# One decoder layer on one core: attention scores made for four heads at a time, value products in turns over two banks, the last result in two halves

## The chip, the cores and the metric

The kernel runs on one of the eight cores of a Trainium2 chip. The metric is the device time of one execution in microseconds (us). TensorE (PE) multiplies matrices, VectorE (DVE) and ScalarE (ACT) do elementwise work, GpSimd (POOL) does small arithmetic and issues the accumulating loads, SyncE (SP) issues the other loads and the stores. Each engine takes its instructions in the order in which they were written.

## What is computed

One layer on 256 tokens of width 1024, all in float32 (cut to what matters):

```
h = rms_norm(x, norm1_g); proj = h @ w_in
q, k, v, u = split(proj, [512, 1024, 1536])            # 8 heads of 64
q, k = rope(rms_norm(q, q_norm_g)), rope(rms_norm(k, k_norm_g))
p = softmax(where(key <= query, q @ k.T / 8, -inf))    # one block of 256 keys: causal attention
attn = p @ v
conv = silu(layer_norm(causal_depthwise_conv(glu(u + glu_b), dw_w) + dw_b))
x = x + concat(attn, conv) @ w_out
h = rms_norm(x, norm2_g)
y = x + (silu(h @ w_gate) * (h @ w_up)) @ w_down       # width 2816
```

## The kernel before

**Products and weights.** Each float32 product is made of three: both factors are split into a high part (`h`, rounded to 12 bits of mantissa) and a rest (`l`), and hi*hi, hi*lo and lo*hi are added in one PSUM bank. Weights come from memory as blocks `raw` (SP's queue); ACT writes `wh` (line 270), DVE writes `wl` (line 275), as pieces of 1024 columns, seven of which may be alive.

**Order.** Nothing is reordered by a scheduler: the program is recorded in the order in which Python writes it. The loop over the input projection has five chunks of 512 columns (k, q, gate, conv input, v), each with eight steps of six products (line 686, two banks `p`). At each step `step()` runs the side tasks that have become due, and `yield n` puts a task off by n steps; so what a task issues stands on every engine between the products of two steps.

**Attention.** `q_task` ends by spawning four `pair_task`s, three steps apart. A pair makes the scores `S` of two heads (line 525): for each head a 128x128 and a 128x256 product with 64 rows, the two heads in different halves of the rows of the array (64 rows x 128 columns) and in two banks (tag `s`, two buffers). One step later `head_task` masks (line 534, a custom DVE instruction that adds the mask, and reads out the row maximum `mx`), makes the bias `bi` (line 538, with `scq`, made by POOL), waits, lets ACT take exponentials `p` (line 543), DVE normalizes (`rec` line 549, `p` line 551), PE transposes (`pT`, line 555), ACT copies to `pTs` (line 557). The transposed `p` of all heads meet the values `vs` (lines 693 and 694, ACT) in `O` (line 706): 16 products of 64 columns each, the two heads of a pair in two halves of the columns of the array, pair after pair, token half after token half. `O` has a bank for four heads; `split` (lines 251 and 252) turns each bank into `mixh` and `mixl`.

**Behind it.** Convolution in a transformed domain (`hf`, `cv`), its normalization (`ln_task`, transposes `cT`), the output projection (`po`, line 724), second normalization with transposes `x2T`, the feed-forward part (`fg`, `U`, `V`, `W`, transposes `aT`), the down projection `pd`. The last four rows of `pd` are finished one output tile at a time; DVE adds the residual (`o`, line 953) and SP's queue stores it (line 954), four times 128x512.

**Banks.** PSUM has eight: tag `mm` four (`p`, `O`, `po`, `fg`, `pd`), `s` two (`S`, `hf`, `cv`, `U`, `V`), `t` two (transposes and others). A tile takes the buffer of its tag that was used longest ago, and its first writer waits until that one's last reader is done.

Of the kernel before, what the change touches and what calls it, by code (L numbers as in the profile page):

```python
# [8 lines left out]
F32 = mybir.dt.float32  # L9
# [4 lines left out]
ALU = mybir.AluOpType  # L14
AX = mybir.AxisListType

P = 128
D = 1024
T = 256
NT = T // P  # L20
KT = D // P
W = 512
H = 8
HD = 64
# [25 lines left out]
KT_WAIT = 3  # L50
S_WAIT = 4
LATE = (1, 5)
GLU0_WAIT = 3
L1 = 8
L2 = 28
# [135 lines left out]
def _build(nc, tc, t, ctx):  # L191
# [6 lines left out]
    early_ctx = ExitStack()  # L198
    early = early_ctx.enter_context(tc.tile_pool(name="early", bufs=1))

    def mm_bank(name, cols=512):
        return psum.tile([P, cols], F32, name=name, tag="mm", bufs=4)

    def t_bank(name, tag="t"):
        return psum.tile([P, 512], F32, name=name, tag=tag, bufs=2)

    def work(name, tag, bufs, shape=(P, W), dt=F32):
        return early.tile(list(shape), dt, name=name, tag=tag, bufs=bufs)
# [12 lines left out]
    def spawn(gen, wait=0):  # L221
        tasks.append([now[0] + wait, gen])
# [263 lines left out]
    def q_task(banks):  # L486
        kqT = keep.tile([P, 2, 4, T], F32, name="kqT", tag="x2T")
        G["kT"], G["qT"] = kqT[:, 0], kqT[:, 1]
        qr, totals = [], []
        for i in range(NT):  # L490
            t1, total = rope_half(banks[i], 0, i, "q")
            totals.append(total)
            qr.append(t1)
            if i == 0:
                yield Q_GAP
        spawn(transposed(qr, G["qT"], "q"), QT_WAIT)
        yield 1
        for i in range(NT):
            r3 = heads3(G["kr"][i])
            nc.vector.tensor_tensor(r3, r3, cqk[1][:, i, :, None].to_broadcast([P, H, HD]), op=ALU.mult)  # L500
        spawn(transposed(G["kr"], G["kT"], "k"), KT_WAIT)
        yield 1
        for total in totals:
            total()
        mean_square(0)
        root(late_part)
        G["scq"] = early.tile([P, NT, H], F32, name="scq")
        nc.gpsimd.tensor_scalar(G["scq"], cqk[0], HD ** -0.5, None, op0=ALU.mult)
        for name, shape in (("fwd", [P, 2, NT, T]), ("ends", [96, R3 - 1]), ("inv", [P, 2, 3, T])):
            tl = early.tile(shape, F32R, name=name)  # L510
            nc.gpsimd.dma_start(tl, t[name])
            G[name] = tl if name == "ends" else (tl[:, 0], tl[:, 1])
        yield S_WAIT
        G["sums"] = early.tile([P, NT, H], F32, name="sums")
        G["pT"] = [None] * H
        for j in range(H // 2):
            spawn(pair_task(j), 3 * j)

    def pair_task(j):

        banks = [t_bank(f"S{2 * j + a}", "s") for a in range(2)]
        for out, q, k in ((slice(0, P), slice(0, P), slice(0, P)), (slice(P, 3 * P), slice(P, T), slice(0, T))):
            for a in range(2):
                rows = slice(a * HD, (a + 1) * HD)
                nc.tensor.matmul(banks[a][:, out], G["qT"][rows, j, q], G["kT"][rows, j, k], start=True, stop=True)  # L525
        for a in range(2):
            spawn(head_task(2 * j + a, banks[a], a), 1)
        yield 0

    def head_task(h, S, odd):  # L530
        sm = work(f"sm{h}", "sm", 3, shape=(P, 3 * P))
        mx = work(f"mx{h}", "mx", 4, shape=(P, NT))
        for i in range(NT):
            nc.vector.tensor_tensor_reduce(out=sm[:, spl[i]], in0=S[:, spl[i]], in1=mask[:, spl[i]], op0=ALU.add,  # L534
                                           op1=ALU.max, scale=1.0, scalar=-3e38, accum_out=mx[:, i:i + 1])
        bi = work(f"bi{h}", "bi", 4, shape=(P, NT))
        scq = G["scq"]
        nc.vector.scalar_tensor_tensor(bi, mx, -1.0, scq[:, :, h], op0=ALU.mult, op1=ALU.mult)
        yield HEAD_EXP + odd
        p = work(f"p{h}", "p", 3, shape=(P, 3 * P))  # L540
        s = G["sums"][:, :, h]
        for i in range(NT):
            nc.scalar.activation(p[:, spl[i]], sm[:, spl[i]], AF.Exp, bias=bi[:, i:i + 1], scale=scq[:, i, h:h + 1],
                                 accum_out=s[:, i:i + 1])
        if h == H - 1:
            nc.scalar.activation(table, one, AF.Silu)
        yield 1
        rec = work(f"rec{h}", "rec", 2, shape=(P, NT))
        nc.vector.reciprocal(rec, s)
        for i in range(NT):  # L550
            nc.vector.tensor_scalar(p[:, spl[i]], p[:, spl[i]], rec[:, i:i + 1], 1.0, op0=ALU.mult, op1=ALU.mult)  # L551
        yield 3 if h in LATE else 2
        b = t_bank(f"pT{h}")
        for a in range(3):
            nc.tensor.transpose(b[:, a * P:(a + 1) * P], p[:, a * P:(a + 1) * P], ident)  # L555
        G["pT"][h] = work(f"pTs{h}", f"pTs{h}", 1, shape=(P, 3 * P))
        nc.scalar.activation(G["pT"][h], b[:, 0:3 * P], AF.Copy)
# [114 lines left out]
    after = (k_task, q_task, gate_task, conv_task, None)  # L672
    unit = 0
    for chunk in range(5):
        banks = [mm_bank(f"p{chunk}{i}") for i in range(NT)]
        for kt in range(KT):
            step()
            feed(unit // 2 + 1 if unit < L1 else (unit + 3) // 2 if unit < L2 else min(unit // 2 + 3, BEHIND))
            w = wtile(unit * W, W)
            unit += 1  # L680
            sls = [slice(i * P, (i + 1) * P) for i in range(NT)]
            order = [(i, a) for i in range(NT) for a in range(3)]
            if W_FIRST < unit <= SWAP:
                order = [(0, 0), (0, 2), (1, 0), (1, 2), (0, 1), (1, 1)]
            for i, a in order:
                nc.tensor.matmul(banks[i], (xh, xh, xl)[a][:, kt, sls[i]], w[a % 2], start=kt == 0 and a == 0,  # L686
                                 stop=kt == KT - 1 and a == 2 - (order[-1][1] == 1))
        if after[chunk]:
            spawn(after[chunk](banks))
# [4 lines left out]
    nc.scalar.activation(vs[:, 1, :], banks[1], AF.Copy, scale=rstd1[:, 1:2])  # L694
    G["third"]()
    mix = G["mix"] = [keep.tile([P, KT, T], F32R, name="mix" + s, tag="big_" + s) for s in "hl"]
    O = [None, None]
    for pair in range(H // 2):
        step()
        if pair % 2 == 0:  # L700
            O[pair // 2] = mm_bank(f"O{pair // 2}").rearrange("p (a q) -> p a q", a=2)
        for i in range(NT):
            for odd in range(2):
                h = 2 * pair + odd
                o = O[pair // 2][odd * HD:(odd + 1) * HD, pair % 2, i * P:]
                nc.tensor.matmul(o, vs[:, i, h * HD:(h + 1) * HD], G["pT"][h][:, i * T:i * T + T - i * P],  # L706
                                 start=i == 0, stop=i == 1)
        if pair % 2:
            sl = slice(pair - 1, pair + 1)
            split([m[:, sl, :] for m in mix], O[pair // 2], nc.vector)  # L710
    spawn(ln_task())


# [46 lines left out]
    for k in range(4):  # L760
        feed(at + LEAD)
        for i in range(NT):
            for n in range(2):
                if k == 0:
                    po[i, n] = mm_bank(f"po{i}{n}")
                product(po[i, n], [m[:, k, tok(i)] for m in mix], wpart(at, n), k == 0, False)
        at += 1
    early_ctx.close()
# [123 lines left out]

    def plain_unit(c, z, kh, half):
        if kh == half == 0:
            banks[z] = [mm_bank(f"fg{c}{z}{i}") for i in range(NT)]
        for k in (2 * half, 2 * half + 1):
            for i in range(NT):
                product(banks[z][i], [a[:, 4 * kh + k, tok(i)] for a in g], wpart(at, k % 2),
                        kh == k == 0, kh == 1 and k == 3)
        if kh == half == 1:  # L900
            if WIDTHS[c] == W:
                spawn((gate2_task, up2_task)[z](c, banks[z], W), EVICT)
            else:
                spawn(gate2_task(c, banks[0], T), EVICT)
                spawn(up2_task(c, banks[0], T), EVICT + 1)
# [19 lines left out]

    def row(f, i, n, w):
        if f == 0:
            pd[i, n] = mm_bank(f"pd{i}{n}")
        product(pd[i, n], [acts[:, z, f, tok(i)] for z in range(2)], w, f == 0, f == NF - 1)

    spawn(norm2_task(), SS_WAIT)
# [16 lines left out]
    for i in range(NT):  # L948
        for n in range(2):
            for f in range(NF - LAST, NF):  # L950
                row(f, i, n, wpart(last[f], n))
            o = late.tile([P, W], F32, name=f"o{i}{n}", tag="sum", bufs=4)
            nc.vector.tensor_tensor(o, pd[i, n], x2[:, i, n * W:n * W + W], op=ALU.add)
            nc.sync.dma_start(t["out"][i][:, n * W:n * W + W], o)


def _layout(a):
# [56 lines left out]
```

## Time and profile before

| what | us |
|---|---|
| time, median of 3 runs (lowest, highest) | 285.69 (285.67, 286.34) |
| time of the profiled execution | 285.98 |
| its span in the trace | 284.2 |
| PE busy | 278.0 |
| DVE busy | 238.6 |
| ACT busy | 189.0 |
| POOL busy | 30.5 |

The span runs from the program's first instruction to its last. The 1.78 us by which the profiled execution is longer than its span lie outside the program's instructions and are taken as fixed. A timeline row has: start, time from the first start to the last end, engine, line, operation, output<-inputs, shapes, how many instructions are merged in it, and in brackets the idle time of the engine before it with what ended it. A product's end is modelled and lies after the start of the next one, so distances on PE are counted from start to start. A float32 product (`S`, `O`) makes two records.

### The profile page before, as it was taken

The numbers are of one execution on the slowest core, as the hardware profiler recorded it, in microseconds if no ns is written. First come the engines' busy times: TensorE is split into PE (matmuls) and PEld (weight loads), VectorE is DVE, ScalarE is ACT, GpSimd is POOL, SyncE is SP. The second block draws the span as 40 slices with busy tenths as digits, with TensorE's granted clock in tenths as the row PEclk, the third lists the DMA queues.
The fourth block names the chain that finished last, engine by engine and source line by source line (L and its number), as shares of the span: only waits on it lengthen the run. The fifth ranks groups of instructions, "written<-read, shape, count | busy, mean of one in ns | idle before, by whom it ended". The sixth has DMA issues, their size and how long they took to land.

```text
span 284.2 us, 3708 instructions
## 1 busy us (share of the span) xinstructions
PE 278.0 (98%) x1302; PEld 226.2 (80%) x1302; DVE 238.6 (84%) x352; ACT 189.0 (67%) x280; POOL 30.5 (11%) x54
## 2 busy tenths in 40 slices
PE   8999999999999999999999999999999999999993
PEld 6878877778788888888888888888888888888882
DVE  3889994999994957999998999899997999977421
ACT  5868568978747778664887559765687459864300
POOL 0004565002000000001200112002110022000000
PEclk9999999999999999999999999999999999999999
DMA  7999957834643589247999699996599985900011
GB/s 250 412 414 335 406 187 257 283 138 128 279 149 148 187 302 399 107 191 204 255 254 367 253 211 192 357 423 206 93 212 423 383 158 95 344 12 2 0 74 75
DMA packets 12885, 65.12 MB, mean 229 GB/s; under 512 B 1825, under 2 KB 2433, under 8 KB 7106
## 3 DMA queue, kind: packets, MB, share of 16 engines
q1 hardware_dynamic: 9874, 54.93, 50.9%
q0 software_dynamic: 2848, 9.94, 18.6%
q8 instruction: 10, 0.16, 0.2%
q14 instruction: 9, 0.07, 0.1%
q10 hardware_dynamic: 144, 0.00, 0.0%
HBM read 63.63 MB, written 1.05 MB: 228 GB/s over the span
## 4 chain that ended last, share of the span: by engine, by line
PE 93%; DVE 3%; ACT 1%; issue 0%; DVEq 0%
PE pd L724 21%; PE p L686 16%; PE U L724 15%; PE fg L724 12%; PE po L724 8%; PE V L724 8%; PE W L724 4%; PE aT L805 2%; PE warm L339 1%; DVE wl L275 1%; PE O L706 1%; DVE p L551 1%; DVE sm L534 1%; PE pT L555 1%; PE S L525 1%; PE x2T L747 1%
## 5 line engine op out<-in xcount | busy, mean ns | idle before, releaser
L270 ACT ACTIVATE wh<-raw 128x1024 fp32r<-128x1024 f32 x114 | 117.7, 1057 | 35.8 <-DVE raw L269 20.1
L275 DVE TENSOR_TENSOR wl<-raw,wh 128x1024 fp32r<-128x1024 f32 x114 | 135.9, 1220 | 4.8 <-ACT wh L270 3.8
L724 PE MATMUL pd<-wh,act 128*128 128x512 f32 x176 | 58.0, 394 | 0.0
L724 PEld LDWEIGHTS pd<-wh,act 128*128 128x128 f32 x176 | 33.0, 188 | 6.8
L724 PE MATMUL pd<-wl,act 128*128 128x512 f32 x88 | 34.3, 389 | 0.0
L686 PE MATMUL p<-wh,xh 128*128 128x512 f32 x80 | 32.8, 410 | 0.0
L686 PE MATMUL p<-wh,xl 128*128 128x512 f32 x80 | 31.5, 393 | 0.0
L283 POOL DMA_DIRECT2D raw<-w x16 | 14.1, 880 | 158.4 <-PE fg L724 61.4
L724 PE MATMUL fg<-wh,g 128*128 128x512 f32 x96 | 30.4, 391 | 0.0
L686 PE MATMUL p<-wl,xh 128*128 128x512 f32 x80 | 26.7, 395 | 0.0
L724 PE MATMUL U<-wh,g 128*128 128x512 f32 x64 | 21.5, 393 | 0.0
L724 PEld LDWEIGHTS fg<-wh,g 128*128 128x128 f32 x96 | 18.0, 188 | 3.7
L269 DVE TENSOR_TENSOR raw<-raw,raw 128x1024 f32<-128x1024 f32 x16 | 19.5, 1219 | 0.1
L724 PEld LDWEIGHTS pd<-wl,act 128*128 128x128 f32 x88 | 16.6, 188 | 3.3
L724 PE MATMUL fg<-wl,g 128*128 128x512 f32 x48 | 18.7, 390 | 0.0
L686 PEld LDWEIGHTS p<-wh,xh 128*128 128x128 f32 x80 | 15.3, 191 | 3.7 <-issue 0.7
L686 PEld LDWEIGHTS p<-wl,xh 128*128 128x128 f32 x80 | 15.1, 189 | 3.4 <-DVE wl L275 0.4
L686 PEld LDWEIGHTS p<-wh,xl 128*128 128x128 f32 x80 | 15.1, 189 | 3.1
L808 ACT ACTIVATE act<-aT 128x512 fp32r<-128x512 f32 (+1 forms) x12 | 6.7, 560 | 12.8 <-PE aT L805 12.8
L724 PEld LDWEIGHTS U<-wh,g 128*128 128x128 f32 x64 | 12.0, 188 | 2.4
L724 PE MATMUL po<-wh,mixh 128*128 128x512 f32 x32 | 12.6, 395 | 0.0
L724 PE MATMUL po<-wh,mixl 128*128 128x512 f32 x32 | 12.5, 390 | 0.0
(184 smaller groups left out, 445.9 us busy)
## 6 DMA issues: line engine op xcount, KB each, us to landing
raw<-w SPq DMA_DIRECT2D x45, 1024.0 KB, 7.0
raw<-w POOLq DMA_DIRECT2D x16, 512.0 KB, 7.0
first<-first SPq DMA_DIRECT2D x8, 384.0 KB, 6.0
xtok<-xtok SPq DMA_DIRECT2D x2, 512.0 KB, 9.1
x<-xtok SPq DMA_DIRECT2D x2, 512.0 KB, 6.5
out<-o SPq DMA_DIRECT2D x4, 256.0 KB, 2.0
inv<-inv POOLq DMA_DIRECT2D x1, 768.0 KB, 9.5
c_glub<-glub SPq DMA_DIRECT2D x1, 512.0 KB, 10.1
```

The lines of the kernel that those rows point to most:

```text
L269: nc.vector.tensor_tensor(src, src, blocks[add][:, cut(a)], op=ALU.add)
L270: nc.scalar.activation(dst[0], src, AF.Copy)
L275: nc.vector.tensor_tensor(dst[1], src, dst[0].bitcast(F32), op=ALU.subtract)
L283: nc.gpsimd.dma_start(blocks[to][:, cut(a)], t["w"][more - 2][:, cut(a)], accum_op=ALU.add)
L339: nc.tensor.matmul(warm[:, 0:T], zeros[:, 0:P], zeros, start=True, stop=True)
L525: nc.tensor.matmul(banks[a][:, out], G["qT"][rows, j, q], G["kT"][rows, j, k], start=True, stop=True)
L534: nc.vector.tensor_tensor_reduce(out=sm[:, spl[i]], in0=S[:, spl[i]], in1=mask[:, spl[i]], op0=ALU.add, op1=ALU.max, scale=1.0, scalar=-3e ...
L551: nc.vector.tensor_scalar(p[:, spl[i]], p[:, spl[i]], rec[:, i:i + 1], 1.0, op0=ALU.mult, op1=ALU.mult)
L686: nc.tensor.matmul(banks[i], (xh, xh, xl)[a][:, kt, sls[i]], w[a % 2], start=kt == 0 and a == 0, stop=kt == KT - 1 and a == 2 - (order[-1] ...
L724: nc.tensor.matmul(bank, l, r, start=start and a == 0, stop=stop and a == 2, skip_group_check=on)
L805: nc.tensor.transpose(b[:, a, :], u[:, a * P:(a + 1) * P], ident)
L808: nc.scalar.activation(hi, b[:, 0:nf, :], AF.Copy)
```

## The change

- The four `pair_task`s become two `pairs_task`s, of four heads each, three steps apart. The second pair of heads in each takes its two banks from the tag `mm0`. The masks of four heads stand together, then their four biases. There are eight buffers each of `sm`, `mx` and `bi` (before 3, 4 and 4). `head_task` begins with the exponentials, and is put off so that ACT issues them at the same places as before.
- The tag `mm` with four buffers becomes `mm0` and `mm1` with two each. Chunks of the projection take them by turns, both `O` banks are of `mm1`, `po` of token half 0 of `mm0` and so on.
- `O`: both banks from the start, and of each turn first the four products of token half 0 (both banks), then those of half 1; both banks are split at the end.
- The last of the four output tiles is added and stored in two halves of 256 columns, the second half by ACT's queue.
- The buffer for descriptors of POOL's loads is set to 8192.

```diff
+SECOND = 3
+SCORES = 8
+SCRATCH = 8192
-    def mm_bank(name, cols=512):
-        return psum.tile([P, cols], F32, name=name, tag="mm", bufs=4)
+    def mm_bank(name, two):
+        return psum.tile([P, 512], F32, name=name, tag=f"mm{two}", bufs=2)
...
-        for j in range(H // 2):
-            spawn(pair_task(j), 3 * j)
+        spawn(pairs_task(0))
+        spawn(pairs_task(2), SECOND)
+        for h in range(H):
+            spawn(head_task(h), 3 * (h // 2) + h % 2 + HEAD_EXP + 1 + (h < 2))
+
+    def pairs_task(first):
+        banks = {}
+        for j in (first, first + 1):
             for a in range(2):
+                banks[2 * j + a] = t_bank(f"S{2 * j + a}", "s") if j == first else mm_bank(f"S{2 * j + a}", 0)
+            for out, q, k in ((slice(0, P), slice(0, P), slice(0, P)), (slice(P, 3 * P), slice(P, T), slice(0, T))):
+                for a in range(2):
+                    rows = slice(a * HD, (a + 1) * HD)
+                    nc.tensor.matmul(banks[2 * j + a][:, out], G["qT"][rows, j, q], G["kT"][rows, j, k],
+                                     start=True, stop=True)
+        yield 1
+        mx = {}
+        for h, S in banks.items():
+            sm = masked[h] = work(f"sm{h}", "sm", SCORES, shape=(P, 3 * P))
+            mx[h] = work(f"mx{h}", "mx", SCORES, shape=(P, NT))
+            for i in range(NT):
+                nc.vector.tensor_tensor_reduce(out=sm[:, spl[i]], in0=S[:, spl[i]], in1=mask[:, spl[i]], op0=ALU.add,
+                                               op1=ALU.max, scale=1.0, scalar=-3e38, accum_out=mx[h][:, i:i + 1])
+        for h in banks:
+            bias[h] = work(f"bi{h}", "bi", SCORES, shape=(P, NT))
+            nc.vector.scalar_tensor_tensor(bias[h], mx[h], -1.0, G["scq"][:, :, h], op0=ALU.mult, op1=ALU.mult)
         yield 0
...
-    for pair in range(H // 2):
+    O = [mm_bank(f"O{n}", 1).rearrange("p (a q) -> p a q", a=2) for n in range(2)]
+    for second in range(2):
         step()
...
+        for i in range(NT):
+            for n in range(2):
+                for odd in range(2):
+                    h = 4 * n + 2 * second + odd
...
+        step()
+    for n in range(2):
+        split([m[:, 2 * n:2 * n + 2, :] for m in mix], O[n], nc.vector)
...
-            nc.vector.tensor_tensor(o, pd[i, n], x2[:, i, n * W:n * W + W], op=ALU.add)
-            nc.sync.dma_start(t["out"][i][:, n * W:n * W + W], o)
+            parts = 2 if i and n else 1
+            for a in range(parts):
+                one = slice(a * W // parts, (a + 1) * W // parts)
+                all_ = slice(n * W + one.start, n * W + one.stop)
+                nc.vector.tensor_tensor(o[:, one], pd[i, n][:, one], x2[:, i, all_], op=ALU.add)
+                (nc.scalar if a else nc.sync).dma_start(t["out"][i][:, all_], o[:, one])
```

On PE, in chunk 3, before (`S_530` and `S_531` are heads 0 and 1, `S_570` and `S_571` heads 2 and 3; `pw` is a product of the convolution's taps):

```order
L433 MATMUL pw_527<-dws,tapr 128x512
L525 MATMUL S_530<-kqT 128x128
L525 MATMUL S_531<-kqT 128x128
L525 MATMUL S_530<-kqT 128x256
L525 MATMUL S_531<-kqT 128x256
L686 MATMUL p_509<-wh_409,xh 128x512
```

and now, with heads 2 and 3 as `S_536` and `S_537`:

```order
L436 MATMUL pw_527<-dws,tapr 128x512
L533 MATMUL S_530<-kqT 128x128
L533 MATMUL S_531<-kqT 128x128
L533 MATMUL S_530<-kqT 128x256
L533 MATMUL S_531<-kqT 128x256
L533 MATMUL S_536<-kqT 128x128
L533 MATMUL S_537<-kqT 128x128
L533 MATMUL S_536<-kqT 128x256
L533 MATMUL S_537<-kqT 128x256
L698 MATMUL p_509<-wh_409,xh 128x512
```

Heads 2 and 3 have moved up behind heads 0 and 1; in the same way heads 4 to 7 now stand where heads 2 and 3 stood, and nothing is left at the two later places.

On DVE, behind the masks of heads 0 and 1, before:

```order
L538 SCALAR_TENSOR_TENSOR bi_562<-mx_559,scq 128x2
L275 TENSOR_TENSOR wl_537<-raw_303,wh_536 128x1024
L549 RECIPROCAL rec_591<-sums 128x2
L551 TENSOR_SCALAR p_576<-p_576,rec_591 128x128
L551 TENSOR_SCALAR p_576<-p_576,rec_591 128x256
L534 ISA sm_598,mx_599<-S_570,c_mask 128x128
```

and now, behind the masks of heads 0 to 3 (`S_588` is head 4, `S_595` head 7, `rec_639` head 0):

```order
L541 ISA mx_571 128x1
L545 SCALAR_TENSOR_TENSOR bi_574<-mx_559,scq 128x2
L545 SCALAR_TENSOR_TENSOR bi_576<-mx_563,scq 128x2
L545 SCALAR_TENSOR_TENSOR bi_578<-mx_567,scq 128x2
L545 SCALAR_TENSOR_TENSOR bi_580<-mx_571,scq 128x2
L278 TENSOR_TENSOR wl_543<-raw_303,wh_542 128x1024
L541 ISA sm_615,mx_616<-S_588,c_mask 128x128
```

and, at the end of the masks of heads 4 to 7 that follow there,

```order
L541 ISA sm_627,mx_628<-S_595,c_mask 128x256
L541 ISA mx_628 128x1
L545 SCALAR_TENSOR_TENSOR bi_631<-mx_616,scq 128x2
L545 SCALAR_TENSOR_TENSOR bi_633<-mx_620,scq 128x2
L545 SCALAR_TENSOR_TENSOR bi_635<-mx_624,scq 128x2
L545 SCALAR_TENSOR_TENSOR bi_637<-mx_628,scq 128x2
L561 RECIPROCAL rec_639<-sums 128x2
```

All eight masks now stand ahead of the first normalization; in the rest of DVE's order nothing but masks and biases has gone.

On PE, the first value products, before (`pTs_649` and `pTs_696` are heads 0 and 1, `pTs_702` and `pTs_735` heads 2 and 3; 64x256 is token half 0, 64x128 half 1):

```order
L706 MATMUL O_905<-pTs_649,vs 64x256
L706 MATMUL O_905<-pTs_696,vs 64x256
L706 MATMUL O_905<-pTs_649,vs 64x128
L706 MATMUL O_905<-pTs_696,vs 64x128
L706 MATMUL O_905<-pTs_702,vs 64x256
```

and now (`pTs_790` and `pTs_825` are heads 4 and 5, in the other bank):

```order
L717 MATMUL O_897<-pTs_679,vs 64x256
L717 MATMUL O_897<-pTs_714,vs 64x256
L717 MATMUL O_898<-pTs_790,vs 64x256
L717 MATMUL O_898<-pTs_825,vs 64x256
L717 MATMUL O_897<-pTs_679,vs 64x128
```

The first product that reads the second half of `vs` has moved from the third to the fifth place.

More of the change, by code (lines that the diff above doesn't have):

```diff
@@ L515, in q_task @@
         G["pT"] = [None] * H
-        for j in range(H // 2):
-            spawn(pair_task(j), 3 * j)
-    def pair_task(j):
-        banks = [t_bank(f"S{2 * j + a}", "s") for a in range(2)]
-        for out, q, k in ((slice(0, P), slice(0, P), slice(0, P)), (slice(P, 3 * P), slice(P, T), slice(0, T))):
-            for a in range(2):
[L524 to L527, printed above, removed]
-        yield 0
@@ L530, in head_task @@
[L530 to L539, printed above, removed]
+        spawn(pairs_task(0))
@@ L540, in head_task @@
+    masked, bias = {}, {}
+    def head_task(h):
+        sm, bi, scq = masked[h], bias[h], G["scq"]
         p = work(f"p{h}", "p", 3, shape=(P, 3 * P))
@@ L674, in _build @@
     for chunk in range(5):
-        banks = [mm_bank(f"p{chunk}{i}") for i in range(NT)]
+        banks = [mm_bank(f"p{chunk}{i}", chunk % 2) for i in range(NT)]
         for kt in range(KT):
@@ L696, in _build @@
     mix = G["mix"] = [keep.tile([P, KT, T], F32R, name="mix" + s, tag="big_" + s) for s in "hl"]
-    O = [None, None]
-    for pair in range(H // 2):
+    O = [mm_bank(f"O{n}", 1).rearrange("p (a q) -> p a q", a=2) for n in range(2)]
+    for second in range(2):
         step()
-        if pair % 2 == 0:
-            O[pair // 2] = mm_bank(f"O{pair // 2}").rearrange("p (a q) -> p a q", a=2)
         for i in range(NT):
[L703 to L710, printed above, removed]
+            for n in range(2):
+                for odd in range(2):
+                    h = 4 * n + 2 * second + odd
+                    o = O[n][odd * HD:(odd + 1) * HD, second, i * P:]
+                    nc.tensor.matmul(o, vs[:, i, h * HD:(h + 1) * HD], G["pT"][h][:, i * T:i * T + T - i * P],
+                                     start=i == 0, stop=i == 1)
+        step()
+    for n in range(2):
+        split([m[:, 2 * n:2 * n + 2, :] for m in mix], O[n], nc.vector)
     spawn(ln_task())
@@ L764, in _build @@
                 if k == 0:
-                    po[i, n] = mm_bank(f"po{i}{n}")
+                    po[i, n] = mm_bank(f"po{i}{n}", i)
                 product(po[i, n], [m[:, k, tok(i)] for m in mix], wpart(at, n), k == 0, False)
@@ L894, in plain_unit @@
         if kh == half == 0:
-            banks[z] = [mm_bank(f"fg{c}{z}{i}") for i in range(NT)]
+            banks[z] = [mm_bank(f"fg{c}{z}{i}", z) for i in range(NT)]
         for k in (2 * half, 2 * half + 1):
@@ L927, in row @@
         if f == 0:
-            pd[i, n] = mm_bank(f"pd{i}{n}")
+            pd[i, n] = mm_bank(f"pd{i}{n}", 1 - i)
         product(pd[i, n], [acts[:, z, f, tok(i)] for z in range(2)], w, f == 0, f == NF - 1)
@@ L1004 @@
     arrays = {**_layout(inputs), **_constants()}
-    nc = _bacc.Bacc("TRN2", target_bir_lowering=False, num_devices=1)
+    nc = _bacc.Bacc("TRN2", target_bir_lowering=False, num_devices=1,
+                     dynamic_dma_scratch_size=SCRATCH)
     arrays = {k: np.ascontiguousarray(v) for k, v in arrays.items()}
```

## The prediction

> **What bounds the kernel now.** I read the page first, then PE's waits, then PE's timeline at the places that the change touches, then DVE and ACT there, and the end.
>
> ```profile
> PE 278.0 (98%) x1302; PEld 226.2 (80%) x1302; DVE 238.6 (84%) x352; ACT 189.0 (67%) x280; POOL 30.5 (11%) x54
> ...
> PE 93%; DVE 3%; ACT 1%; issue 0%; DVEq 0%
> ```
>
> ```profile
> PE S L525 <- DVE mx L534: 0.3, 1, 0.3
> ```
>
> ```profile
> 80.00:280.00 200.00, 199.28 (x912) 164.72 (x910) 170.28 (x201) 127.70 (x165) 14.08 (x16) 1.00 0.68 214
> ```
>
> PE is the bound from the first product to the last, at a granted clock of 1.00. Its waits for others sum to 0.3 us beside 1.0 us of start. So time is gained only by what PE does not have to do, and by the end behind its last product. DVE (170.28 of 200 us) and ACT (127.70) have spare time in the long second part, so a lead that PE wins early should last. The 98%, though, hide distances between products that are longer than a stream needs: those are what this change can remove.
>
> **Scores: what a pair costs.** PE's timeline around the four pairs and, last, around a transpose without scores. A plain 512-column product starts 0.23 after the one before (57.20 and 57.43 below); one behind a change of shape is late.
>
> ```profile
> 42.08 0.39 PE L433 MATMUL pw<-dws,tapr 96*128 96x512 f32 x1
> 42.40 0.93 PE L525 MATMUL S<-kqT 64*128 64x128 f32 x8
> 43.26 0.50 PE L686 MATMUL p<-wh,xh 128*128 128x512 f32 x1
> 43.59 0.40 PE L686 MATMUL p<-wh,xl 128*128 128x512 f32 x1
> ```
>
> ```profile
> 42.73 0.60 PE L525 MATMUL S<-kqT 64*128 64x256 f32 x4
> ...
> 42.94 0.38 PE L525 MATMUL S<-kqT 64*128 64x256 f32 x2
> ```
>
> ```profile
> 46.45 0.93 PE L525 MATMUL S<-kqT 64*128 64x128 f32 x8
> ...
> 51.07 0.61 PE L686 MATMUL p<-wl,xh 128*128 128x512 f32 x2
> 51.62 0.93 PE L525 MATMUL S<-kqT 64*128 64x128 f32 x8
> 52.47 0.55 PE L555 MATMUL pT<-c_ident,p 128*128 128x128 f32 x3
> ...
> 53.09 0.39 PE L686 MATMUL p<-wh,xl 128*128 128x512 f32 x1
> ...
> 57.20 0.39 PE L686 MATMUL p<-wl,xh 128*128 128x512 f32 x1
> 57.43 0.39 PE L686 MATMUL p<-wh,xl 128*128 128x512 f32 x1
> 57.75 0.48 PE L525 MATMUL S<-kqT 64*128 64x128 f32 x2
> 58.50 0.92 PE L525 MATMUL S<-kqT 64*128 64x128 f32 x6 [0.26 <-DVE mx L534]
> 59.35 0.55 PE L555 MATMUL pT<-c_ident,p 128*128 128x128 f32 x3
> ...
> 59.96 0.39 PE L686 MATMUL p<-wl,xh 128*128 128x512 f32 x1
> ...
> 62.27 0.39 PE L686 MATMUL p<-wh,xl 128*128 128x512 f32 x1
> 62.50 0.49 PE L555 MATMUL pT<-c_ident,p 128*128 128x128 f32 x3
> ...
> 63.06 0.39 PE L686 MATMUL p<-wl,xh 128*128 128x512 f32 x1
> ```
>
> First pair: from `pw` (42.08) to the second `p` behind the scores (43.59) are 1.51; without scores it would be two plain distances, 0.46. The pair costs 1.05. Of this, streaming is 0.63: the two passes over 256 columns start 0.21 apart (42.73, 42.94), so those over 128 columns need half, and each pass serves both heads at once, 2x0.21 + 2x0.105. The other 0.42 is the price of going into this shape of the array and out again: 0.09 ahead of the first score, 0.11 for its first weights, 0.11 behind the last, 0.11 at the first `p`. The second pair has the same row (0.93) and is taken as equal, 1.05. The third: 51.07 begins two products, so the stream without it goes on at 51.53; to 53.09 are 1.56, less the 0.56 that a transpose and a product take without scores (62.50 to 63.06): 1.00. The fourth: 57.66 to 59.96 are 2.30, less 0.56: 1.74. It stops in its middle, since head 7's bank is free only when DVE has masked head 5, and the two heads then no longer run side by side. Together 4.84.
>
> Now there are two groups of four heads, each with the price of one shape change: 2 x (1.05 + 0.63) = 3.36. **Gain 1.48.** Above, nothing in the trace lets it be more than the whole overhead, 4.84 - 4x0.63 = 2.3; below, none of the shape price saved and only the stall gone, 0.7.
>
> In the Trainium skill, "TensorEngine Tiling (Array Packing)", Key Properties, changing the tiling mode drains the array; it lists no exposed weight load. By this rule alone two changes less would save only the two drains each (0.09 and 0.11 in the rows above), 0.4, and with the stall the gain would be about 1.1. I stay with the rows' 0.42.
>
> **Does the order still feed PE?** DVE's rows that set the pace, and two transposes on PE:
>
> ```profile
> 43.36 0.29 DVE L534 CUSTOM_DVE_ANT_0 sm<-S,c_mask 128x128 f32<-128x128 f32 x1 [0.16 <-PE S L525]
> ...
> 43.57 0.42 DVE L534 CUSTOM_DVE_ANT_0 sm<-S,c_mask 128x256 f32<-128x256 f32 x1
> 43.92 0.08 DVE L534 DVE_READ_ACCUMULATOR2_ANT mx<- 128x1 f32 x1
> ...
> 45.70 1.22 DVE L275 TENSOR_TENSOR wl<-raw,wh 128x1024 fp32r<-128x1024 f32 x1
> ...
> 49.42 0.17 DVE L549 RECIPROCAL rec<-sums 128x2 f32<-128x2 f32 x1 [2.50 <-ACT p L543]
> ...
> 54.73 0.55 DVE L551 TENSOR_SCALAR p<-p,rec 128x128 f32<-128x128 f32 x2
> ```
>
> ```profile
> 55.63 0.81 PE L555 MATMUL pT<-c_ident,p 128*128 128x128 f32 x6
> ```
>
> A head's mask takes 0.56 (43.36 to 43.92), so four take 2.2 to 3.0, the upper end with a bias after each. They end at 45.6 to 46.4; `wl` follows with its four biases at 46.0 to 46.8 instead of 45.70. The second group of scores starts at 47.1 (46.45 plus the 0.63 that the first has grown) and needs the banks of heads 0 to 3: free, with 0.7 to spare at worst. Its masks run from 48.1 to 50.3 or 51.1, in the 2.50 us in which DVE was idle; head 0's normalization moves from 49.4 to 50.8 or so, and DVE is back on its old times at about 54, where it lacks the masks that stood later. What is late next is the exponentials: ACT stands behind the last `pw`, which comes 0.63 later, so `p` of head 2, normalized at 55.28 before (54.73 plus 0.55), is ready near 55.9, when its transpose, second of the six at 55.63 and then 0.3 later, is due at 56.26. The cover has shrunk to about 0.3, and for heads 3 and 4 it is no more. I cost this at nothing, with up to 0.6 for the range.
>
> Bank names change, but each tile still follows the same one as before except `S` of heads 2, 3, 6, 7, which stand between gate and v chunks in `mm0`; v starts behind the six transposes of 55.63, over 4 us after the last mask. POOL's smaller buffer: zero; POOL's loads keep their order, and POOL was busy for 14.08 of 200 us.
>
> **Value products.** Weight loads for `O`, ACT's `vs`, and PE:
>
> ```profile
> 73.89 0.20 PEld L706 LDWEIGHTS O<-pTs,vs 128*64 128x64 f32 x4 [0.38 <-ACT vs L693]
> 74.50 0.20 PEld L706 LDWEIGHTS O<-pTs,vs 128*64 128x64 f32 x4 [0.41 <-ACT vs L694]
> ```
>
> ```profile
> 73.76 0.69 ACT L694 ACTIVATE vs<-p,c 128x512 f32<-128x512 f32 x1
> ```
>
> ```profile
> 74.16 0.39 PE L706 MATMUL O<-pTs,vs 128*64 128x256 f32 x2
> ...
> 76.82 0.50 PE L293 MATMUL cv<-yh,inv 128*128 128x512 f32 x1
> ```
>
> The second pass starts at 74.16, and the next product could at 74.37; it waits for the second half of `vs` (ready at 74.45) until 74.50: 0.13, and its weights are then loaded in the open, 0.05. With four products of half 0 first the need moves to 74.79, behind 74.45. **Gain 0.18**, between 0 and 0.18; streaming is the same. Both splits come behind the products, about 0.7 later for the first bank, under the sixteen `cv` products that PE has next, 0.23 each: nothing.
>
> **The end.**
>
> ```profile
> 279.32 0.69 DVE L953 TENSOR_TENSOR o<-pd,x 128x512 f32<-128x512 f32 x1 [2.03 <-PE pd L724]
> ```
>
> ```profile
> 280.04 0.33 SPq L954 DMA_DIRECT2D out<-o  x1
> ```
>
> ```profile
> DMA to landing us min/median/max: 2.0/2.0/3.2
> ...
> SPq L1009 <- DMA out<-o: 2.4, 1, 2.4
> ```
>
> The last store is issued at 280.04 and, as SP's wait of 2.4 shows, it is the one that took 3.2. The first half's sum takes about 0.42 (as the 256-column mask), so its store goes 0.27 earlier; the second half's sum ends about 0.07 later than now, but its store has half the bytes and a queue of its own. Bounds: -0.1 (the second lands as late after its issue as now) to 1.5 (it lands in 1.7, and the 1.2 over the median does not recur). I take **0.3**, near the lower end, since the median store took 2.0 and halving can only touch the part of that which moves bytes.
>
> [...] No row before shows a store of 128 KB.
>
> **Sum.** 1.48 + 0.18 + 0.3 = 1.96. The profiled execution (285.98) would come to 284.0; it stands 0.29 above the median of the runs, and from that median, 285.69, it is 283.7. A difference under 0.3% (0.86 us) is about what cannot be told from no change.
>
> **Rivals.**
> - The end gives nothing: the half stores are still bound by what follows the last byte. For it: 2.0 for every store, whatever came before. 284.0. Chance 0.17.
> - The end gives all: the 3.2 was chance or is broken by the halves, 282.5. For it: the median; against: the runs lie at 285.67 and 285.69 without it being seen that they had it. Chance 0.13.
> - Transposes wait for `p`: the cover of 0.3 above is gone at heads 2 to 4, since ACT and DVE are later than I walked them; 0.6 lost, 284.3. If the lead is also lost later, where `aT` or `pd` wait for DVE, 285.2, no change. Chances 0.12 and 0.09.
> - Slower: the second group of scores stands at the head of PE and needs the banks of heads 0 to 3. Heads 6 and 7 are due at 47.7; if DVE's masks of heads 2 and 3 ended at 49.7 instead of 46.4, PE would have lost the 1.96, and from 50.6 on the kernel is slower, 286.6 and up. Against it: all that stands ahead of them on DVE is two masks. Chance 0.04.
> - The forecast itself: 0.45.
>
> **Chances and range.** Faster by over 0.3% are the forecast, both ends and waiting transposes: 0.87, of which I leave 0.04 to what these rows don't show: 0.83. No change 0.12, slower 0.05. The range 282.3 to 284.9 holds the forecast, both ends and the waiting transposes; left out are the lost lead and the slower case.
>
> **What would show it.** Right: PE's score rows come twice, x16, each about 1.6 long, and no wait for `mx`; `cv` starts about 1.6 earlier than 76.82; `O` has no wait for line 694; the last sum starts near 277.7 instead of 279.32. Wrong: a wait of `pT` for `p` or `pTs`, a second group of scores that starts after 47.7, `cv` early but `pd`'s end not, or a last store that lands over 3 us after its issue.

## The result, and the profile after

| | before | after |
|---|---|---|
| median of six runs, us | 285.73 (285.05 to 286.34) | 283.07 (282.36 to 283.77) |
| ratio, 95% interval | | 0.9907 (0.9887 to 0.9927) |
| profiled run, us | 285.98 | 282.85 |
| its span, us | 284.2 | 281.1 |

Faster by 2.7 us, 0.9%; 283.7 was forecast, 282.3 to 284.9. The page after, its engines and its chain that ended last:

```profile
PE 276.5 (98%) x1302; PEld 225.8 (80%) x1302; DVE 238.5 (85%) x353; ACT 188.6 (67%) x280; POOL 30.5 (11%) x54
...
PE 92%; DMA 4%; DVE 1%; issue 1%; SPq 0%; ACT 0%; DVEq 0%
```

The same 1302 products, 1.5 us less of PE's time. DVE has one instruction more, 353 for 352: the second half of the last sum. (The expectations below count 451 and 450, since they include records that the page leaves out.) This one instruction turns out to matter. PE's waits after, all of them:

```profile
PE warm L342 <- DVE one L325: 1.0, 1, 1.0
```

The wait of `S` for `mx` is gone and no wait of a transpose for `p` has come. The scores on PE's timeline after:

```profile
41.99 0.39 PE L436 MATMUL pw<-dws,tapr 96*128 96x512 f32 x1
42.31 1.58 PE L533 MATMUL S<-kqT 64*128 64x128 f32 x16
43.83 0.50 PE L698 MATMUL p<-wh,xh 128*128 128x512 f32 x1
44.16 0.39 PE L698 MATMUL p<-wh,xl 128*128 128x512 f32 x1
...
46.49 0.62 PE L698 MATMUL p<-wl,xh 128*128 128x512 f32 x2
47.04 1.58 PE L533 MATMUL S<-kqT 64*128 64x128 f32 x16
48.55 0.50 PE L698 MATMUL p<-wh,xh 128*128 128x512 f32 x1
48.89 0.40 PE L698 MATMUL p<-wh,xl 128*128 128x512 f32 x1
...
52.81 0.49 PE L567 MATMUL pT<-c_ident,p 128*128 128x128 f32 x3
```

By the prediction's own subtraction the first group costs 44.16 - 41.99 - 0.46 = 1.71. Behind 46.49 come two products, so the stream without scores would go on at 46.95; 48.89 - 46.95 - 0.23 = 1.71 for the second. Together 3.42 for 4.84 before: 1.42 gained.

The value products and the product behind them, on PE:

```profile
72.03 0.40 PE L627 MATMUL hf<-tail,ends 96*120 96x512 f32 x1
72.36 2.82 PE L717 MATMUL O<-pTs,vs 128*64 128x256 f32 x32
75.11 0.50 PE L296 MATMUL cv<-yh,inv 128*128 128x512 f32 x1
```

`cv` starts at 75.11 where it stood at 76.82: 1.71 earlier. From here to the last product the distance to the kernel before stays the same; the lead is not lost. The end after: the two last sums, one row on DVE's timeline,

```profile
277.62 0.76 DVE L968 TENSOR_TENSOR o<-pd,x 128x256 f32<-128x256 f32 x2 [2.03 <-PE pd L735]
```

their stores with size and time from issue to landing,

```profile
out<-o SPq DMA_DIRECT2D x1, 128.0 KB, 1.8
out<-o ACTq DMA_DIRECT2D x1, 128.0 KB, 1.8
```

and what SP waited for (in all, times, longest):

```profile
SPq L1025 <- DMA out<-o: 1.2, 2, 0.9
```

The last sum starts 1.70 earlier than before, but the span is 3.1 shorter. From the start of the last sum to the end of the span it was 284.2 - 279.32 = 4.9; it is 281.1 - 277.62 = 3.5. So 1.4 us of the 3.1 came from the end, for which 0.3 was forecast. That is the difference to explain.

### The profile page after: what moved, and what is told of

It is laid out like the page before. It is cut to its first block, busy times and chain, and to the rows that moved or that the text cites. A ratio compares the mean times of both kernels' runs of the same rounds, so it can differ in the third digit from the quotient of the medians.

```text
span 281.1 us, 3712 instructions
## 1 busy us (share of the span) xinstructions
PE 276.5 (98%) x1302; PEld 225.8 (80%) x1302; DVE 238.5 (85%) x353; ACT 188.6 (67%) x280; POOL 30.5 (11%) x54
## 3 DMA queue, kind: packets, MB, share of 16 engines
HBM read 63.63 MB, written 1.05 MB: 230 GB/s over the span
## 4 chain that ended last, share of the span: by engine, by line
PE 92%; DMA 4%; DVE 1%; issue 1%; SPq 0%; ACT 0%; DVEq 0%
PE pd L735 21%; PE U L735 16%; PE p L698 15%; PE fg L735 12%; PE po L735 8%; PE V L735 8%; PE W L735 4%; DMA c_gqk<-gqk 3%; PE aT L816 2%; DMA first<-first 1%; PE S L533 1%; PE O L717 1%; PE pT L567 1%; PE x2T L758 1%; PE cv L296 0%
```

## The experiments

Two questions: do the scores gain through fewer changes of the array's shape or through the removed stall alone; and what brought 1.4 us at the end.

### The end: one piece or two

`e1_tail_one` is the changed kernel with its last result in one piece:

```diff
-            parts = 2 if i and n else 1
+            parts = 1
```

`e2_tail_alone` is the kernel before with the new end (`parts`, two sums, two stores) and nothing else. `e5_halves_sp` is the changed kernel with both halves on SP's queue:

```diff
-                (nc.scalar if a else nc.sync).dma_start(t["out"][i][:, all_], o[:, one])
+                nc.sync.dma_start(t["out"][i][:, all_], o[:, one])
```

> The changed kernel with its last result in one piece again (one add of 512 columns, one store of 256 KB on SP's queue); scores and value products stay changed. Theory A (the halves bring what the end gained): the last add starts at about 277.6 as in the changed kernel, the last store lands 3.2 us after its issue as before the change, and the run takes 1.0 to 1.4 us more than the changed kernel: 284.1 to 284.5, ratio to the kernel before about 0.995. Rival B (the 3.2 us was one engine's late packet that has nothing to do with the halves): the store lands in 2.0 us, the end loses 0.15 us at most, 283.0 to 283.3, ratio 0.991.

> The kernel before with the last result in two halves (second half stored by ACT) and nothing else changed. Theory A: the span falls by 1.0 to 1.4 us, 284.3 to 284.7, ratio about 0.996, landing of the last stores 1.8 to 2.3 us; nothing ahead of the last add moves. Rival B: by the issue and landing of ordinary stores (before: 0.69 of add and 2.0 to land; halves: 0.76 and 1.8) the gain is 0.15 us at most, 285.5 to 285.8, ratio 0.9995, unless the late packet goes elsewhere by chance.

> The changed kernel with both halves of the last result stored by SP. If the second queue matters: the second store is issued 0.1 to 0.4 us later, behind the first one's 0.33 us of issue, and the time is 283.2 to 283.5, ratio 0.9915 to 0.9925. If only the halving matters: 283.0 to 283.1, ratio 0.9907, landing 1.8 us for each. If neither matters (the late packet's chance): landing anything between 1.8 and 3.2.

Measured: `e1` 284.16 (ratio 0.9945, 0.9929 to 0.9960), 1.1 over the changed kernel; `e2` 284.27 (0.9956, 0.9940 to 0.9972); `e5` 282.93 (0.9908, 0.9892 to 0.9923). The times follow theory A, halves gain over 1 us, and the queue makes no difference that they can show. The profile does not follow it: in `e1` the last store, whole again, landed in 2.4, not 3.2. Its last sum, and its four stores of 256 KB:

```profile
277.55 0.69 DVE L968 TENSOR_TENSOR o<-pd,x 128x512 f32<-128x512 f32 x1 [2.03 <-PE pd L735]
```

```profile
DMA to landing us min/median/max: 2.0/2.0/2.4
```

From the last sum to the end `e1` takes 281.7 - 277.55 = 4.1; with the 2.0 of the median store it would be 3.7. `e1`'s profiled run was the fastest of its six (283.47; the others 283.88 to 284.26). Something hits the last store, and by these times it varies from run to run. In a narrow window over the DMA queues (queue and kind: packets, MB, share of the 16 engines) it has a name. The kernel before, 281.8 to 281.9, with its last sum at 279.32 and its last store issued at 280.04:

```profile
q14 instruction: 1, 0.01, 19.3%
```

A packet of the instruction queue: a piece of a program is being fetched, 1.8 us after the last store was issued. In `e1` it comes at 280.1 to 280.2, again 1.8 after the issue. The changed kernel has the packet too, at 276.0 to 276.1, ahead of its last sum:

```profile
q14 instruction: 1, 0.01, 32.4%
```

`e2` has it there (277.5, last sum 279.06), `e5` too (276.2, last sum 277.79). All these differ from the others by halves, but also by DVE's 353rd instruction.

### The end: one instruction more, one less

`e6_dve_one` is the kernel before with a needless instruction at its very start, and `e10_one_shifted` is `e1` with the same:

```diff
     nc.vector.memset(one, 1.0)
+    spare_one = const.tile([P, 1], F32, name="spare_one")
+    nc.vector.memset(spare_one, 0.0)
```

`e9_dve_less` is the changed kernel, halves and all, with one less, and `e7_sp_one` the kernel before with a small transfer more on SP:

```diff
-    one = const.tile([P, 1], F32, name="one")
-    nc.vector.memset(one, 1.0)
+    one = zeros[:, 0:1]
```

```diff
         nc.sync.dma_start(x2[:, i, :], t["xtok"][i])
+    spare_g = keep.tile([P, KT], F32, name="spare_g")
+    nc.sync.dma_start(spare_g, t["g1"])
```

> The kernel before, its last result still in one piece, with one needless VectorE instruction more at its very start (a memset of 128x1 that nothing reads). Theory C (the late landing of the last store is the fetch of VectorE's next piece of program, an 8192-byte packet of the instruction queue, which falls after the last add in programs with 450 VectorE records and after the add before it in those with 451): the fetch moves to about 277.6 us, the last store lands in 2.0 us, and the kernel gets faster by about 1.2 us from one instruction more: 284.4 to 284.8, ratio 0.9958. Rival D (SP's program is what is fetched, or the halves themselves bring the gain): nothing moves, 285.6 to 286.0, ratio 1.000, the fetch still at 1.83 us after the issue of the last store.

> The kernel before with one needless transfer of 4 KB more on SP's queue in the middle of the program (128x8, nothing reads it), so one or two more instructions of SP. Theory C: the fetch stays behind the last store, no change, 285.6 to 286.1, ratio 1.000 to 1.001. Rival D (SP's program is what is fetched): the fetch moves ahead of the last store and the kernel takes 284.4 to 284.8, ratio 0.9958.

> The changed kernel, halves and all, with one VectorE instruction less at its start (the memset of the constant 1, whose only readers are the two needless activations that load tables; they read a zero instead), so 450 VectorE records like the kernel before. Theory C (the count of VectorE's instructions decides when the last piece of program is fetched): the 8192-byte packet goes back behind the last add, the last store lands late, and the kernel is 0.4 to 1.2 us slower than the changed one for one instruction less: 283.5 to 284.2, ratio 0.993 to 0.9955. Rival (the halves avoid the late landing by themselves): as the changed kernel, 282.9 to 283.1, ratio 0.9907, the packet at 276.1.

> The changed kernel with its last result in one piece and one needless VectorE memset more at the start (451 VectorE records like the changed kernel). Theory C: the packet comes ahead of the last add, the store of 256 KB lands in 2.0 to 2.2 us, the span from the last add to the end is 3.73 us as in the kernel before with that memset (changed kernel: 3.46), 283.3 in all, ratio 0.9917; so the halves themselves are worth 0.27 us and the rest of the gain at the end was the packet. Rival (the halves are worth about 1 us): 284.1 as with the one piece without the memset, ratio 0.9945.

`e6`: 284.72 against 285.46 for the kernel before beside it, ratio 0.9977 (0.9966 to 0.9987): less than the 1.2 expected, but faster by 0.7 us from one useless instruction. Its last sum, its packet in the window from 277.5 to 277.6, its four stores:

```profile
279.17 0.69 DVE L955 TENSOR_TENSOR o<-pd,x 128x512 f32<-128x512 f32 x1 [2.03 <-PE pd L726]
```

```profile
q14 instruction: 1, 0.01, 30.0%
```

```profile
DMA to landing us min/median/max: 2.0/2.0/2.2
```

PE's products stand where they stood, within 0.2; the packet has gone from 281.8 to 277.5, and the end takes 282.9 - 279.17 = 3.7 for 4.9. `e9`: 283.81, ratio 0.9937 (0.9915 to 0.9960), with the packet at 279.7 to 279.8. Its last sums, and in the DMA queues the packet and the two half stores:

```profile
277.49 0.76 DVE L967 TENSOR_TENSOR o<-pd,x 128x256 f32<-128x256 f32 x2 [2.03 <-PE pd L734]
```

```profile
q14 instruction: 1, 0.01, 23.3%
...
out<-o SPq DMA_DIRECT2D x1, 128.0 KB, 1.8
out<-o ACTq DMA_DIRECT2D x1, 128.0 KB, 2.9
```

Halves do not avoid it: with 352 instructions the packet is back, the second half lands in 2.9, and the end takes 282.0 - 277.49 = 4.5. `e10`: 283.05 (282.84 to 283.47, four runs; a fifth, of 1594 us, is left out), ratio 0.9918 (0.9902 to 0.9935), packet at 276.0 to 276.1. Its last sum, and SP's wait for the stores:

```profile
277.37 0.69 DVE L970 TENSOR_TENSOR o<-pd,x 128x512 f32<-128x512 f32 x1 [2.03 <-PE pd L737]
```

```profile
SPq L1027 <- DMA out<-o: 1.2, 1, 1.2
```

One piece, and as fast as the changed kernel: its end takes 281.1 - 277.37 = 3.7. Against `e1`, the same kernel without the memset, that is 1.1 us in the medians. `e7` left the packet behind the last store (283.4 to 283.5, last sum 280.85), so a longer program of SP does not move it. Its time, 286.72 (1.0046, 1.0031 to 1.0060), is a miss of both expectations: PE's products are 0.8 later already at 33 us, long before the added transfer (issued at 72.2), and 1.5 later at the end. Why is open; the added tile may move others in memory, which wasn't tried.

| kernel | last result | DVE instructions | packet | last sum to end of span |
|---|---|---|---|---|
| before | one piece | 352 | behind | 4.9 |
| `e1` | one piece | 352 | behind | 4.1 |
| `e9` | halves | 352 | behind | 4.5 |
| `e7` | one piece | 352 | behind | 4.1 |
| `e6` | one piece | 353 | ahead | 3.7 |
| `e10` | one piece | 353 | ahead | 3.7 |
| after | halves | 353 | ahead | 3.5 |
| `e2` | halves | 353 | ahead | 3.4 |
| `e5` | halves, one queue | 353 | ahead | 3.6 |
| `e3` | halves | 353 | ahead | 3.4 |
| `e4` | halves | 353 | ahead | 3.5 |
| `e8` | halves | 353 | ahead | 3.4 |

In all twelve profiles here (`e3`, `e4` and `e8` are described below) the packet is behind the last sum where DVE has 352 instructions, and ahead of it where it has 353. Halves stand on both sides, and the changed kernel differs from `e1` without an added tile. The halves by themselves are worth 0.2 to 0.3 (3.7 against 3.4 and 3.5), which the medians of `e10` and the changed kernel cannot show; the packet is worth 0.4 to 1.2 by profiles, 0.7 to 1.1 by medians.

The traces also show how the packet lengthens the end. A store ends with sixteen updates of its semaphore. In the kernel before, the last store's data had all moved by 281.87 and fifteen updates had come by 282.04; the sixteenth came at 283.21. SP's queue, from 282.1 to 282.2, has one packet left, which started as the instruction packet ended (282.17):

```profile
q1 hardware_dynamic: 1, 0.00, 0.6%
```

In `e9` too the store's last packet started behind the instruction packet, and the sixteenth update came 1.1 after the fifteenth. In `e1` and `e7` it started just ahead, and the sixteenth update was 0.4 late. With the packet out of the way (`e6`, `e10`) it was late by 0.03 at most. That the two packets share one of the 16 engines is inferred from this.

### The scores: four groups, two, one

`e3_four_groups` is the changed kernel with a group for each pair, the banks `s` and `mm0` in turns, so that nothing stalls:

```diff
-        spawn(pairs_task(0))
-        spawn(pairs_task(2), SECOND)
+        for j in range(H // 2):
+            spawn(pairs_task(j), (1, 2, SECOND, SECOND + 1)[j])
...
-        for j in (first, first + 1):
+        for j in (first,):
-            banks[2 * j + a] = t_bank(f"S{2 * j + a}", "s") if j == first else mm_bank(f"S{2 * j + a}", 0)
+            banks[2 * j + a] = t_bank(f"S{2 * j + a}", "s") if j % 2 == 0 else mm_bank(f"S{2 * j + a}", 0)
```

> The changed kernel with the scores in four groups of two heads between the product units, each with banks of its own, so that no score product waits for a bank; the masks run by pairs. Own theory (each entry into the scores' tile shape and back costs about 0.42 us of TensorE beside 0.63 of streaming a pair): the first transposes of p start 0.84 us later than in the changed kernel (53.65 instead of 52.81), 283.9 in all, ratio 0.9937. Rival (the gain came from the removed stall of 0.7 and two pairs' overlap of weight loads alone, an entry costs at most the 0.1 of one exposed load): 0 to 0.2 us later, 283.1 to 283.3, ratio 0.991 to 0.9915.

283.47, ratio 0.9925 (0.9910 to 0.9940). PE's timeline:

```profile
41.59 0.39 PE L436 MATMUL pw<-dws,tapr 96*128 96x512 f32 x1
41.91 0.93 PE L533 MATMUL S<-kqT 64*128 64x128 f32 x8
...
43.10 0.40 PE L698 MATMUL p<-wh,xl 128*128 128x512 f32 x1
...
48.92 0.62 PE L698 MATMUL p<-wl,xh 128*128 128x512 f32 x2
49.48 0.93 PE L533 MATMUL S<-kqT 64*128 64x128 f32 x8
...
50.67 0.40 PE L698 MATMUL p<-wh,xl 128*128 128x512 f32 x1
...
53.23 0.49 PE L567 MATMUL pT<-c_ident,p 128*128 128x128 f32 x3
```

From `pw` to the first transpose are 53.23 - 41.59 = 11.64; in the changed kernel 52.81 - 41.99 = 10.82. So 0.82 for two shape changes, as expected (0.84); the whole run is only 0.4 over the changed kernel's, since its scores began 0.4 earlier: a gap of that size, at 20 us on PE in the changed kernel's profile, is not in this one. The first pair costs 43.10 - 41.59 - 0.46 = 1.05, the last 50.67 - 49.38 - 0.23 = 1.06, and the two between the same: about 4.23, against 4.84 before with the stall and 3.42 in two groups. The gain of 1.42 is thus 0.61 of stall and 0.81 of shape changes, and the rival, the stall alone, has fallen. The reading by which a change costs its drains alone has fallen too: it came to 0.4 for the two changes. In the Trainium skill, "TensorEngine Tiling (Array Packing)", Key Properties, changing the tiling mode drains the array; the 0.09 us ahead of the first score (42.31 - 41.99 - 0.23 in the changed kernel) agrees with it, and the whole price is 0.41 for each group.

`e8_one_group` puts all eight heads in one group, with the parts of several heads in one bank:

```diff
+        first = [t_bank(f"SA{a}") for a in range(2)]
+        last_ = [mm_bank(f"SB{a}", 0) for a in range(2)]
+        diag = [t_bank(f"SD{a}", "s") for a in range(2)]
...
+                S[2 * j + a] = (diag[a][:, j * P:(j + 1) * P],
+                                (first, last_)[j // 2][a][:, j % 2 * T:j % 2 * T + T])
```

> The changed kernel with the scores of all eight heads in one group: the 256-column parts of two heads share a bank, the 128-column parts of four heads share one, six banks in all; masks, exponents and everything behind keep their order. Own theory (0.41 us per entry into the scores' tile shape and back, as four groups against two showed with 0.82): one entry less, the first transposes of p start 0.41 us earlier against the start of the scores than in the changed kernel, 282.65 in all, ratio 0.9893. Rival (the stretch between the groups hid something that the one group lays open: the next product waits for t's banks, or the weights' parts come late since VectorE's masks wait for the longer group): no gain or up to 0.5 us lost, 283.1 to 283.6, ratio 0.991 to 0.9925.

284.50, ratio 0.9972 (0.9958 to 0.9986): by the medians 1.4 slower than the changed kernel; own theory missed, and the rival was too mild. On PE, among its weight loads with ACT's row that they wait for, on DVE, and in PE's waits:

```profile
41.95 0.49 PE L536 MATMUL SD<-kqT 64*128 64x128 f32 x4
42.27 0.91 PE L536 MATMUL SA<-kqT 64*128 64x256 f32 x3
...
45.30 0.50 PE L702 MATMUL p<-wh,xh 128*128 128x512 f32 x1
```

```profile
42.06 0.60 ACT L437 ACTIVATE Ws<-pw 128x512 f32<-128x512 f32 x1 [1.02 <-PE pw L436]
42.70 0.18 PEld L536 LDWEIGHTS SA<-kqT 64*128 64x128 f32 x1 [0.24 <-ACT Ws L437]
```

```profile
44.77 0.29 DVE L545 CUSTOM_DVE_ANT_0 sm<-SD,c_mask 128x128 f32<-128x128 f32 x1 [2.25 <-PE SD L536]
```

```profile
PE pT L571 <- DVE p L567: 0.7, 2, 0.4
```

The group starts at 41.95 and the next product at 45.30, 3.35 later. A group of two pairs takes 43.83 - 42.31 = 1.52 in the changed kernel, so four should take 1.52 + 2x0.63 = 2.8. Early in the group one head's product of 256 columns came 0.2 behind its partner's (in the row x3 instead of x2), and the two ran out of step to the end. The weight loads name the wait: the two `SA` banks are of tag `t`, whose other user here is `pw`, the product just ahead, and ACT copied `pw` out only from 42.06 to 42.66. In the changed kernel no score takes a bank of `t`. Of the 0.55 by which the group is longer than 2.8 this wait is 0.2; that the rest comes from being out of step is not shown apart. And the first mask waits for `SD`, each bank of which now holds parts of four heads, nearly to the end of the group: it starts at 44.77, in the changed kernel at 43.27. That delay runs through the exponentials to the transposes, which then wait for `p`. The price per shape change still stands by `e3`; one group gives it away again through its banks.

### The values' products

`e4_o_pairs` is the changed kernel with the old order of the value products, pair by pair and half by half:

> The changed kernel with the values' products pair by pair again, each pair first token half 0 and then 1, and the split of a bank right behind its second pair; scores and end stay changed. Own theory (the old order's second product waits for the second half of vs, 0.18 us): the wait for vs is back as two waits in the weight loads, the products take 3.0 instead of 2.82 us, the first product of cv starts 0.18 us later against the start of the products, and the time is 0.18 us over the changed kernel's. Rival (vs is no limit there, the 0.18 us came from elsewhere): no difference in that stretch.

A single run, 283.45, which cannot settle 0.18 in the time. PE, and the weight loads with the wait for the second half of `vs`:

```profile
72.44 0.40 PE L627 MATMUL hf<-tail,ends 96*120 96x512 f32 x1
72.78 3.00 PE L716 MATMUL O<-pTs,vs 128*64 128x256 f32 x32
75.70 0.50 PE L296 MATMUL cv<-yh,inv 128*128 128x512 f32 x1
```

```profile
73.38 2.15 PEld L716 LDWEIGHTS O<-pTs,vs 128*64 128x64 f32 x28 [0.41 <-ACT vs L706]
```

From `hf` to `cv` are 3.26, in the changed kernel 75.11 - 72.03 = 3.08: 0.18, with that wait back.

## Why the prediction was right, and where its size was off

- **Scores, 1.48 forecast, 1.42 measured.** Fewer shape changes 0.81 (0.84 forecast), stall 0.61. The second group started at 47.04 (47.1 forecast) and found its banks free. Head 2's transpose did not wait: its `p` was normalized by 55.71, and the six transposes began at 55.90.
- **Value products, 0.18 forecast, 0.18 measured** (`e4`).
- **The lead kept.** The products behind `cv` kept their 1.71; neither `aT` nor `pd` gave it back.
- **The end, 0.3 forecast, 1.4 measured in the profile.** This is the term that was mis-sized: "I take 0.3, near the lower end, since the median store took 2.0". For what halving does, that was right: 0.2 to 0.3. But the 3.2 us of the last store was taken for the store's own, or for chance, and it was neither. A fetch of program fell behind it, and the added half sum, by being one instruction more on DVE, moved the fetch ahead. The rival "the end gives all" (282.5) named the size and not the reason. The first rival, that the end gives nothing, fell, though its premise nearly stood: whole stores land in 2.0 and halves in 1.8.
- **The sum.** By the profiles 1.42 + 0.18 + 1.4 and 0.1 of earlier start make the 3.1 by which the span fell; in the medians 2.7, which fits a packet that does not cost the full 1.2 in each run (`e6`: 0.7). `e9`, with all the edits of the change but the old count of instructions, took 283.81, beside the 283.7 that was forecast; the 0.7 that the changed kernel has beyond it came with the count and was luck. The smaller buffer for POOL's loads was not run alone, and the sum leaves nothing for it.

In the Trainium skill, "DMA: Bandwidth & Descriptors", Rules for kernel authors, two transfers to halves of the partitions are called not worth it, since both use the same engines. The halves here are of the columns, on all partitions, so the rule does not name them, but they bring little too: `e10`, in one piece, and the changed kernel have the same median. Had the end been tried alone, as in `e2` against the kernel before, the halves would have looked worth 1.5 us.

## What to carry to other kernels

Price a change of the array's shape by the distance of the products around it, not by the engine's busy share (98% throughout): here 0.41 us for each way in and out. In `e8` one more of them was saved and nothing gained: its banks were shared, and one of them was not free. When the last store lands later than its like, look in the DMA queues for what shares its last microsecond before crediting an edit of the store. And when an edit changes the number of instructions, run it once with a needless instruction more and once with one less: a gain that follows the count is not the edit's.

## What the runs showed of the hardware that was not expected

- An 8192-byte packet of the instruction queue, fetched behind the last store, lengthened the end by 0.4 to 1.2 us in the profiles; with one DVE instruction more, even at the program's start, it came some 4 us earlier, where it held up at most the store before the last (2.5 us to land in `e10`), which was done before the last one. DVE's count moved it (`e6`, `e9`, `e10`) and an added SP transfer did not (`e7`); that it is DVE's program is inferred from this, and why one instruction moves it by so much is open.
- Two heads that share the array ran in step in the changed kernel, where no score waited for a bank; in `e8` one was held for 0.2 us by a bank that ACT was still reading, they stayed out of step for the rest of the group, and eight heads took 3.35 us instead of 2.8.
- A store of 128 KB landed in 1.8 us, one of 256 KB in 2.0: half the bytes saved 0.2.
